# A hybrid encoder layer: attention scores and value products in fewer, larger groups between projection matmuls

## The chip, the cores and the metric

The kernel runs on one core of a Trainium2 chip. The metric is the device time of one execution in microseconds (us), the median of several runs. An execution is profiled too; its times are counted from the start of its span.

## The reference

One post-norm layer over 512 tokens of width 1024: a token mixer of two parallel branches (a bidirectional Mamba-2 SSD, and dilated sliding-window attention), a gated merge, a LayerNorm, then a squared-ReLU channel layer. What matters here is the attention branch: three groups of four heads of 64, with (window, dilation) of (128, 1), (512, 4) and (2048, 16).

```python
u = h @ w_in
z, xbc, dt_f_raw, dt_b_raw, q, k, v, gate_logits = split(u)
y_ssd = ssd_branch(z, xbc, ...) @ w_proj_ssd
y_att = attention_branch(q, k, v) @ w_proj_attn
gates = sigmoid(gate_logits + b_gate)
mix = (gates[:, :, 0] * y_ssd + gates[:, :, 1] * y_att) @ w_out
h = layer_norm(alpha * h + mix, ln1_g, ln1_b)
...
# attention, for each pattern: scores inside the window, softmax, values
scores = einsum(q, k) / sqrt(64) - slope * distance      # masked by the window
m = max(scores); p = exp(scores - m); den = sum(p)
o = einsum(p, v) / den;  lse = m + log(den)
# the j-th heads of the three patterns are combined by softmax(lse)
y = sum(softmax(lse) * o)
```

## The kernel before

Everything is float32. A large product splits its operands into a high and a low float32r half and runs as three matmuls of 128x128 by 128x512; `quarters` (L160) emits the 24 of one such tile, and gives the turn away after every six. Small products (scores, values, transposes) use plain float32, and the profile shows two records for each such matmul, or for a transpose one.

The order on TensorE is written out by hand: `run(a, b, ta, tb)` takes two generators, counts the units that each yields, and steps the one that is behind its share. So a `yield 3.5` in a generator sets how many projection matmuls stand behind that piece. The orders of VectorE, ScalarE and of SP's DMA queue come from a scheduler, in which some helpers (the splits of weights among them, L110 and L111) have a high priority.

In the first stage `ssd(g)`, for g = 0 to 3, runs beside the input projection (tiles ps_z, ps_x, ps_k, ps_g and so on). Each group builds transposes, six states (ps_st, whose running states pv are made by L711), then pauses, runs `norm` of the group before (ps_ms, L592) and four pairs of heads (ps_yo, L760). A pair's gates G are made on ScalarE and VectorE (L731 to L744), and `y_out` of the next group multiplies them (ps_y, L607).

In the second stage `attention()` runs beside the first half of the SSD output projection (ps_pa), 12 tiles of 24 matmuls.

- Scores of the near pattern (L924): per tile i of two heads, four blocks b of 128 queries. The matmuls have 64 rows, and two heads run at once in the two halves of the array.
- Scores of the other two patterns (L954): per tile of two heads four residue classes r. q and k are loaded from DRAM (L877, L878) into two pairs of buffers that alternate.
- Each score tile is read from PSUM once by VectorE (add of the bias, L932 and L958); then follow the maximum, its negative and ScalarE's exponential with the sum (L936, L964).
- The near statistics go through DRAM to another layout (dr_st, L942, and s, L967). Then the three patterns' weights wg are made, and the near ones w0 go through DRAM too.
- Probabilities are scaled by these weights (L998, L1020), transposed by TensorE (`class_t`, L1001; `near_t`, L1025), copied to SBUF, and multiplied with the values (`class_v`, L1012, 64 columns; `near_v`, L1040, 64 columns, at both ends 64 rows too). The products are put in a list `todo`; `later()` emits what stands in it.

PSUM tiles come from three tags: mm (3 banks, for the projections), tp (3) and y (2). A score tile takes two of tp or two of y, one for each head:

```python
        def pair_tiles(n, name):
            tag, bufs = (("tp", 3), ("y", 2))[n]
            return [ps_tile(tag, f"{name}_{hh}", bufs) for hh in range(2)]
```

After the attention, 24 more projection matmuls run before the first product with its result (ps_pb).

Of the kernel before, what the change touches and what calls it, by code (L numbers as in the profile page):

```python
# [16 lines left out]
P = 128  # L17
# [3 lines left out]
NCH = S // P  # L21
HEADS = 32
GROUPS = 4
HD = 64
# [22 lines left out]
def hybrid_layer_kernel(ctx: ExitStack, tc: tile.TileContext, t: dict, out: bass.AP):  # L47
    nc = tc.nc
    act, dve, pool, pe, dma = nc.scalar, nc.vector, nc.gpsimd, nc.tensor, nc.sync
# [133 lines left out]
    def ps_tile(tag, name, bufs):  # L183
        return psp.tile([P, 512], F32, name=name, tag=tag, bufs=bufs)
# [392 lines left out]
    def square_split(g):  # L577

        sqh = sp.tile([P, S], F32R, name=f"sqh{g}", tag="xw", bufs=1)
        sql = sp.tile([P, S], F32R, name=f"sql{g}", tag="G2", bufs=1)  # L580
        act.copy(sqh, tail[g])
        dve.tensor_sub(sql, tail[g], f32(sqh))
        if not onesr:
            onesr.append(cp.tile([P, P], F32R, name="onesr", tag="dtv", bufs=1))
            act.copy(onesr[0], ones)
        sq_hl[g] = sqh, sql
# [55 lines left out]
    def ssd(g):  # L642
# [23 lines left out]
        for c0 in range(0, NCH, 2):  # L666
            pss = [ps_tile("tp", f"ps_xt{g}_{c}", 3) for c in (c0, c0 + 1)]
# [29 lines left out]
        for n, (i, d, c) in enumerate(steps):  # L697
# [16 lines left out]
                gate(ready[n:n + 1])  # L714
            if n == 4 and g:
                square_split(g - 1)
        yield 2.0 if g < GROUPS - 1 else 5.0
        if g:
            norm(g - 1)

# [145 lines left out]
    def attention():  # L866
# [6 lines left out]
        def tile_qk(n):  # L873
            qk[n] = [(ap if n % 2 else aq).tile([P, S], F32, name=f"{x}{n}", tag=f"{x}{n % 2}", bufs=1) for x in "qk"]

        def load_qk(n):
            dma.dma_start(qk[n][0], dr_qk[n])  # L877
            dma.dma_start(qk[n][1], dr_qk[6 + n])  # L878
# [9 lines left out]
        b12 = ap.tile([P, 8, P], F32, name="b12")  # L888
        ptc = {(gg, jj): ap.tile([P, 4, P], F32, name=f"pt{gg}_{jj}") for gg in range(2) for jj in range(4)}
# [10 lines left out]
        b0 = aq.tile([P, 4, 256], F32, name="b0")  # L900
# [5 lines left out]
        kr = [(max(0, P * b - 64), min(S, P * b + 192)) for b in range(NCH)]  # L906
# [3 lines left out]
# [3 lines that stand above are left out]

        for i in range(2):
            qf, kf = qk[i]
            for bp in range(2):
                pss = pair_tiles(bp, f"ps_s0_{i}{bp}")
                for bb in range(2):
                    b = bp * 2 + bb
                    k0, k1 = kr[b]  # L920
                    o = k0 - (P * b - 64)
                    for hh in range(2):
                        pr = slice(hh * HD, (hh + 1) * HD)
                        pe.matmul(pss[hh][:, bb * 256 + o:bb * 256 + o + k1 - k0], qf[pr, b * P:(b + 1) * P], kf[pr, k0:k1], start=True, stop=True)  # L924
                for hh in range(2):
                    jj = 2 * i + hh
                    for bb in range(2):
                        b = bp * 2 + bb
                        k0, k1 = kr[b]
                        w, o = k1 - k0, k0 - (P * b - 64)  # L930
                        pt = pt0[jj, b]
                        dve.tensor_add(pt[:, :w], pss[hh][:, bb * 256 + o:bb * 256 + o + w], b0[:, jj, o:o + w])  # L932
                        dve.reduce_max(st0[:, b, 0, jj:jj + 1], pt[:, :w], axis=AX.X)
                        nm = nm0[:, b, jj:jj + 1]
                        dve.tensor_scalar(nm, st0[:, b, 0, jj:jj + 1], -1.0, None, op0=ALU.mult)
                        act.activation(pt[:, :w], pt[:, :w], AF.Exp, bias=nm, accum_out=st0[:, b, 1, jj:jj + 1])  # L936
                yield 3.5
        dma.dma_start(vc, dr_v.rearrange("(i r) d -> i r d", r=4)[:, :, 0:512])
        dma.dma_start(v0[:, 1:4, :], dr_v[64:448, 512:768].rearrange("(c p) d -> p c d", p=P))
        dma.dma_start(v0[0:64, 0, :], dr_v[0:64, 512:768])  # L940
        dma.dma_start(v0[0:64, 4, :], dr_v[448:512, 512:768])
        dma.dma_start(dr_st.rearrange("(b p) m -> p b m", p=P), st0.rearrange("p b a j -> p b (a j)"))  # L942
        for gg in range(2):
            for i in range(2):
                tl = 2 + gg * 2 + i
                tile_qk(tl)
                load_qk(tl)
                qf, kf = qk[tl]
                pss = pair_tiles(i, f"ps_s{tl}")
                for r in range(4):  # L950
                    rs = slice(r * P, (r + 1) * P)
                    for hh in range(2):
                        pr = slice(hh * HD, (hh + 1) * HD)
                        pe.matmul(pss[hh][:, rs], qf[pr, rs], kf[pr, rs], start=True, stop=True)  # L954
                for hh in range(2):
                    jj = i * 2 + hh
                    pt = ptc[gg, jj]
                    dve.tensor_add(pt, pss[hh].rearrange("p (r k) -> p r k", r=4), b12[:, gg * 4 + jj:gg * 4 + jj + 1, :].to_broadcast([P, 4, P]))  # L958
                    ms = stc[:, gg, 0, :, jj]
                    dve.reduce_max(ms, pt, axis=AX.X)  # L960
                    nm = nmc[:, gg, jj, :]
                    dve.tensor_scalar(nm, ms, -1.0, None, op0=ALU.mult)
                    for r in range(4):
                        act.activation(pt[:, r, :], pt[:, r, :], AF.Exp, bias=nm[:, r:r + 1], accum_out=stc[:, gg, 1, r, jj:jj + 1])  # L964
                yield 4.0

        dma.dma_start(s0, dr_st.rearrange("(i r) (a j) -> i r a j", r=4, a=2))  # L967
        m = [s0[:, :, 0, :], stc[:, 0, 0], stc[:, 1, 0]]
# [19 lines left out]
        def tt_tile(name):  # L988
            nt[0] += 1
            n = nt[0] % 7  # L990
            if n < 4:
                return (aq, ap)[n // 2].tile([P, 4, P], F32, name=name, tag=("q0", "k0", "q1", "k1")[n], bufs=1)
            return ap.tile([P, 4, P], F32, name=name, tag="tt", bufs=3)

        def class_t(i, hh, gg):
            jj = 2 * i + hh
            pt = ptc[gg, jj]
            dve.tensor_mul(pt, pt, wg[:, 1 + gg, :, jj].unsqueeze(2).to_broadcast([P, 4, P]))  # L998
            ps = ps_tile("tp", f"ps_pt{gg}_{jj}", 3)
            for r in range(4):  # L1000
                pe.transpose(ps[:, r * P:(r + 1) * P], pt[:, r, :], ident)  # L1001
            tt = tt_tile(f"tt{gg}_{jj}")
            act.copy(tt.rearrange("p r q -> p (r q)"), ps)
            return tt

        def class_v(i, ptt):
            pcl[i] = ps_tile("y", f"ps_ac{i}", 2)
            for r in range(4):
                for gg in range(2):
                    for hh in range(2):  # L1010
                        v = vc[:, r, (gg * 2 + i) * P + hh * HD:(gg * 2 + i) * P + (hh + 1) * HD]
                        pe.matmul(pcl[i][hh * HD:(hh + 1) * HD, r * P:(r + 1) * P], v, ptt[hh, gg][:, r, :], start=(gg == 0), stop=(gg == 1))  # L1012
# [3 lines left out]
        def near_t(i, b):  # L1016
            w = kr[b][1] - kr[b][0]
            for hh in range(2):
                pt = pt0[2 * i + hh, b]
                dve.tensor_scalar(pt[:, :w], pt[:, :w], w0[:, b, 2 * i + hh:2 * i + hh + 1], None, op0=ALU.mult)  # L1020
            ps = ps_tile("tp", f"ps_pn{i}_{b}", 3)
            tt = tt_tile(f"tn{i}_{b}")
            for hh in range(2):
                for q, (c0, c1, ck) in enumerate(cuts[b]):
                    pe.transpose(ps[:c1 - c0, (q * 2 + hh) * P:(q * 2 + hh + 1) * P], pt0[2 * i + hh, b][:, c0:c1], ident)  # L1025
            if all(c1 - c0 == P for c0, c1, _ in cuts[b]):
                act.copy(tt.rearrange("p r q -> p (r q)"), ps)
            else:
                for q, (c0, c1, ck) in enumerate(cuts[b]):
                    act.copy(tt[:c1 - c0, 2 * q:2 * q + 2, :], ps[:c1 - c0, q * 256:(q + 1) * 256].rearrange("p (h q) -> p h q", h=2))  # L1030
            return tt
# [21 lines left out]
        def later():  # L1053
            while todo:
                todo.pop(0)()

        for i in range(2):
            tts = {}
            for hh in range(2):
                for gg in range(2):  # L1060
                    tts[hh, gg] = class_t(i, hh, gg)
                    yield 1.4
            later()
            todo.append(lambda i=i, tts=tts: class_v(i, tts))
            for b in range(NCH):
                tt = near_t(i, b)
                yield 2.4
                if b == 2:
                    later()
                todo.append(lambda i=i, b=b, tt=tt: near_v(i, b, tt))  # L1070
        later()

# [111 lines left out]
    for k in range(4):  # L1184
        w = ws.get(2)
# [384 lines left out]
    with tc.manual_schedule(engines={mybir.EngineType.PE}):  # L1570
        for c in range(3):
            for q in range(4):
# [9 lines left out]
                pr = product(c, SEQ[2 * q], ops)  # L1582
# [62 lines left out]
    pss = [bank(n, f"ps_d0_{n}") for n in (3, 4, 5, 2)]  # L1645
    for n in range(4):
        w = ws.get()
# [79 lines left out]
```

## Time and profile before

| what | value |
|---|---|
| median of 3 runs | 982.07 us (981.93 to 982.13) |
| profiled execution, its own time | 982.07 us |
| its span, first to last instruction | 980.3 us |
| TensorE clock granted | 0.997 of full speed |
| attention's scores, 483 to 530 us: TensorE / VectorE / ScalarE busy | 47.00 / 42.15 / 29.49 us |
| attention's values, 530 to 576 us: the same | 46.00 / 17.16 / 17.95 us |
| end of the third SSD group's states, 305 to 320 us: the same | 14.74 / 15.00 / 12.45 us |

Matmuls overlap: one of 512 columns is shown with 0.39 us, and the next starts before it ends. So the busy time of TensorE says little of how densely it works, and starts have to be compared. In the timeline a row has the start, the time from the first start to the last end of the instructions merged in it, the engine, the line, the operation with what it writes and reads, and the count; in brackets stand idle time ahead of it and what ended that.

### The profile page before, as it was taken

The numbers are of one execution on the slowest core, as the hardware profiler recorded it, in microseconds if no ns is written. First come the engines' busy times: TensorE is split into PE (matmuls) and PEld (weight loads), VectorE is DVE, ScalarE is ACT, GpSimd is POOL, SyncE is SP. The second block draws the span as 40 slices with busy tenths as digits, with TensorE's granted clock in tenths as the row PEclk, the third lists the DMA queues.
The fourth block names the chain that finished last, engine by engine and source line by source line (L and its number), as shares of the span: only waits on it lengthen the run. The fifth ranks groups of instructions, "written<-read, shape, count | busy, mean of one in ns | idle before, by whom it ended". The sixth has DMA issues, their size and how long they took to land.

```text
span 980.3 us, 14776 instructions
## 1 busy us (share of the span) xinstructions
PE 971.7 (99%) x5448; PEld 835.2 (85%) x5448; DVE 804.6 (82%) x1247; ACT 607.8 (62%) x1150; POOL 58.7 (6%) x67
## 2 busy tenths in 40 slices
PE   9999999999999999999999999999999999999997
PEld 6988888888888888888778888899999998989986
DVE  7987997688999999997798267498898898898757
ACT  6664795469867985784775343157666666656620
POOL 0100200010001000200000000000200110110000
PEclk9999999999999999999999999999999999999998
DMA  9666466334753575474774247313953754671322
GB/s 350 158 146 172 127 207 192 98 103 150 220 162 106 161 216 149 145 232 134 251 230 155 80 153 271 116 44 130 243 143 136 209 130 172 177 167 44 111 83 86
DMA packets 57992, 155.94 MB, mean 159 GB/s; under 512 B 7488, under 2 KB 10432, under 8 KB 57664
## 3 DMA queue, kind: packets, MB, share of 16 engines
q1 hardware_dynamic: 53072, 139.04, 44.0%
q0 software_dynamic: 4560, 15.44, 8.6%
q8 instruction: 43, 0.70, 0.3%
q10 hardware_dynamic: 288, 0.52, 0.2%
q14 instruction: 29, 0.24, 0.1%
HBM read 128.25 MB, written 12.44 MB: 144 GB/s over the span
## 4 chain that ended last, share of the span: by engine, by line
PE 97%; DVE 1%; issue 1%; DMA 0%; ACT 0%; DVEq 0%; SPq 0%; ACTq 0%
PE ps_pa L160 9%; PE ps_g L160 9%; PE ps_x L160 9%; PE ps_z L160 9%; PE ps_x L1366 8%; PE ps_z L1366 4%; PE ps_q L160 3%; PE ps_k L160 3%; PE ps_u L160 2%; PE ps_pX L170 2%; PE ps_pX L171 2%; PE ps_pX L172 2%; PE ps_yo L760 2%; PE ps_y L1366 2%; PE ps_vX L353 2%; PE ps_pZ L170 2%
## 5 line engine op out<-in xcount | busy, mean ns | idle before, releaser
L111 DVE TENSOR_TENSOR wl<-wraw,wh 128x1024 fp32r<-128x1024 f32 x103 | 126.7, 1234 | 64.0 <-ACT wh L110 48.0
L110 ACT CAST wh<-wraw 128x1024 fp32r<-128x1024 f32 x103 | 107.4, 1046 | 86.7 <-PE ps_o L172 14.0
L1482 DVE TENSOR_TENSOR cl<-wq_B,ch 128x1024 fp32r<-128x1024 f32 x42 | 51.3, 1220 | 14.7 <-ACT ch L1481 14.2
L1481 ACT CAST ch<-wq_B 128x1024 fp32r<-128x1024 f32 x42 | 44.1, 1050 | 24.0 <-PE ps_pX L172 16.6
L160 PE MATMUL ps_pa<-yh,wh 128*128 128x512 f32 x128 | 51.7, 404 | 0.0
L160 PE MATMUL ps_g<-xh,wh 128*128 128x512 f32 x128 | 50.6, 396 | 0.0
L160 PE MATMUL ps_z<-xh,wh 128*128 128x512 f32 x128 | 50.4, 394 | 0.0
L160 PE MATMUL ps_g<-xl,wh 128*128 128x512 f32 x128 | 49.9, 390 | 0.0
L160 PE MATMUL ps_z<-xl,wh 128*128 128x512 f32 x128 | 49.9, 389 | 0.0
L160 PE MATMUL ps_pa<-yl,wh 128*128 128x512 f32 x128 | 48.4, 393 | 0.0
L729 ACT ACTIVATE U<-bc,acr 128x128 f32<-128x128 f32 x128 | 42.2, 390 | 8.3 <-DMA bc<-dr_acr 8.3
L160 PE MATMUL ps_x<-xh,wh 128*128 128x512 f32 x120 | 47.3, 394 | 0.0
L160 PE MATMUL ps_x<-xl,wh 128*128 128x512 f32 x120 | 46.8, 390 | 0.0
L525 DVE SCALAR_TENSOR_TENSOR acc<-ps_x,vec,acc 128x510 f32<-128x510 f32 (+1 forms) x60 | 44.6, 743 | 0.5
L1450 POOL DMA_DIRECT2D wq_B<-wq_B x24 | 20.6, 856 | 402.3 <-DMA wq_B<-in_w_dn_dram 236.4
L731 DVE SCALAR_TENSOR_TENSOR U<-bc,acr,U 128x128 f32<-128x128 f32 x128 | 44.0, 381 | 0.0
L735 ACT ACTIVATE G<-cb,tok 128x128 f32<-128x128 f32 x128 | 41.9, 390 | 0.0
L170 PE MATMUL ps_pX<-ch,ah 128*128 128x512 f32 x96 | 37.6, 392 | 0.0
L171 PE MATMUL ps_pX<-cl,ah 128*128 128x512 f32 x96 | 37.6, 392 | 0.0
L172 PE MATMUL ps_pX<-ch,al 128*128 128x512 f32 x96 | 37.4, 389 | 0.0
L1475 ACT CAST ah<-r 128x1024 fp32r<-128x1024 f32 x21 | 22.1, 1054 | 20.6 <-PE ps_pX L171 14.3
L160 PE MATMUL ps_pa<-yh,wl 128*128 128x512 f32 x128 | 34.8, 392 | 0.0
(884 smaller groups left out, 2825.5 us busy)
## 6 DMA issues: line engine op xcount, KB each, us to landing
wraw<-in_w_in_dram SPq DMA_DIRECT2D x66, 512.0 KB, 3.9
bc<-dr_acr SPq DMA_DIRECT2D x64, 256.0 KB, 4.2
pr<-in_w_up_dram SPq DMA_DIRECT2D x28, 512.0 KB, 5.4
wq_B<-in_w_dn_dram SPq DMA_DIRECT2D x24, 512.0 KB, 4.4
wq_B<-wq_B POOLq DMA_DIRECT2D x24, 512.0 KB, 4.6
be<-dr_ear SPq DMA_DIRECT2D x32, 256.0 KB, 5.3
wraw<-in_w_ps_dram SPq DMA_DIRECT2D x16, 512.0 KB, 3.7
dr_gate<-g SPq DMA_DIRECT2D x16, 256.0 KB, 2.3
```

Of the source, the lines that this page charges most:

```text
L110: a = act.copy(h[:, :width], r[:, :width])
L111: v = dve.tensor_sub(l[:, :width], r[:, :width], f32(h[:, :width]))
L160: ins = pe.matmul(ps, l, r, start=(first and n == 0), stop=(last and n == len(seq) - 1))
L170: pe.matmul(ps, lh, rh, start=(first and i == 0), stop=False, skip_group_check=not check)
L171: pe.matmul(ps, lh, rl, start=False, stop=False, skip_group_check=not check)
L172: ins = pe.matmul(ps, ll, rh, start=False, stop=(last and i == n - 1), skip_group_check=not check)
L525: dve.scalar_tensor_tensor(acc[:, o0:o1], ps[:, i0:i1], w(k), acc[:, o0:o1], op0=ALU.mult, op1=ALU.add)
L729: act.activation(U[:, ch(c)], bb[:, ch(c)], AF.Identity, bias=acr[:, c, 32 + h:33 + h])
L731: dve.scalar_tensor_tensor(U[:, ch(c)], bf[:, ch(c)], acr[:, c, h:h + 1], U[:, ch(c)], op0=ALU.subtract, op1=ALU.min)
L1366: pe.matmul(ps[:, LO], w_[:, wk], src[:, x, k0 + k, cs], start=(first and i == 0), stop=(i == 11), skip_group_check=not first)
L1481: act.copy(h, w[:, j, :])
L1482: dve.tensor_sub(l, w[:, j, :], f32(h))
```

## The change

Four edits. The near scores of one tile are emitted as one group of eight matmuls into four PSUM tiles (before: two groups of four), and the scores of two tiles of the other patterns as one group of 16 (before: two groups of eight). The value products are emitted at two places (before: four): all those of tile 0 behind the second pair of class transposes of tile 1, all those of tile 1 at the end. So that the transposed near blocks can wait that long, they are copied into probability tiles ptc that have been transposed already, not into the rotating tiles. And the pause of the third SSD group is 3.4 units, not 2.0. Line numbers behind the first edit of `attention` move by up to three: the scores are L922 and L956 in the changed kernel.

```diff
-        yield 2.0 if g < GROUPS - 1 else 5.0
+        yield (2.0, 2.0, 3.4, 5.0)[g]
         if g:
             norm(g - 1)
...
         for i in range(2):
             qf, kf = qk[i]
+            pss = [pair_tiles(bp, f"ps_s0_{i}{bp}") for bp in range(2)]
+            for b in range(NCH):
+                k0, k1 = kr[b]
+                o = (b % 2) * 256 + k0 - (P * b - 64)
+                for hh in range(2):
+                    pr = slice(hh * HD, (hh + 1) * HD)
+                    pe.matmul(pss[b // 2][hh][:, o:o + k1 - k0], qf[pr, b * P:(b + 1) * P], kf[pr, k0:k1], start=True, stop=True)
             for bp in range(2):
-                pss = pair_tiles(bp, f"ps_s0_{i}{bp}")
...
-                yield 3.5
+            yield (10.0, 6.5)[i]
...
         for gg in range(2):
+            pss = []
             for i in range(2):
                 tl = 2 + gg * 2 + i
                 tile_qk(tl)
                 load_qk(tl)
+            for i in range(2):
+                tl = 2 + gg * 2 + i
                 qf, kf = qk[tl]
-                pss = pair_tiles(i, f"ps_s{tl}")
+                pss.append(pair_tiles(i, f"ps_s{tl}"))
...
-                yield 4.0
+            yield (8.0, 5.5)[gg]
...
-            tt = tt_tile(f"tn{i}_{b}")
+            tt = ptc[b // 2, 2 * i + b % 2]
...
                 for gg in range(2):
                     tts[hh, gg] = class_t(i, hh, gg)
                     yield 1.4
-            later()
+                if hh == 0:
+                    later()
             todo.append(lambda i=i, tts=tts: class_v(i, tts))
             for b in range(NCH):
                 tt = near_t(i, b)
                 yield 2.4
-                if b == 2:
-                    later()
                 todo.append(lambda i=i, b=b, tt=tt: near_v(i, b, tt))
         later()
```

What this does to the order is shown at three places. First TensorE at the first near scores. Before, four matmuls stand between projection matmuls (ps_s_00 names tile 0, block pair 0, and the last digit the head):

```order
L160 MATMUL ps_pa_4939<-yl_4818,wh_4925 128x512
L924 MATMUL ps_s_00_0_4958<-k_4916,q_4915 128x192
L924 MATMUL ps_s_00_1_4959<-k_4916,q_4915 128x192
L924 MATMUL ps_s_00_0_4958<-k_4916,q_4915 128x256
L924 MATMUL ps_s_00_1_4959<-k_4916,q_4915 128x256
L160 MATMUL ps_pa_4939<-yl_4821,wh_4925 128x512
```

The same place of TensorE in the changed kernel:

```order
L160 MATMUL ps_pa_4939<-yl_4818,wh_4925 128x512
L922 MATMUL ps_s_00_0_4958<-k_4916,q_4915 128x192
L922 MATMUL ps_s_00_1_4959<-k_4916,q_4915 128x192
L922 MATMUL ps_s_00_0_4958<-k_4916,q_4915 128x256
L922 MATMUL ps_s_00_1_4959<-k_4916,q_4915 128x256
L922 MATMUL ps_s_01_0_4960<-k_4916,q_4915 128x256
L922 MATMUL ps_s_01_1_4961<-k_4916,q_4915 128x256
L922 MATMUL ps_s_01_0_4960<-k_4916,q_4915 128x192
L922 MATMUL ps_s_01_1_4961<-k_4916,q_4915 128x192
L160 MATMUL ps_pa_4939<-yl_4821,wh_4925 128x512
```

Block pair 1 has joined pair 0. Before, the eight groups have 12, 18, 12, 12, 18, 18, 12 and 54 projection matmuls behind them; now the four have 42, 24, 30 and 60.

Second, TensorE at the pause of the third SSD group, before:

```order
L160 MATMUL ps_C_3070<-xh_103,wl_2999 128x512
L592 MATMUL ps_ms_3122<-sqh_3084,onesr 128x512
L592 MATMUL ps_ms_3122<-sql_3085,onesr 128x512
L760 MATMUL ps_yo_0_3135<-C_2194,pv_0_1_2929 128x128
L760 MATMUL ps_yo_0_3135<-C_2194,pv_0_2_3013 128x128
L760 MATMUL ps_yo_0_3135<-C_2194,pv_0_3_3081 128x128
L760 MATMUL ps_yo_1_3136<-C_2194,pv_1_0_3104 128x128
```

And in the changed kernel:

```order
L160 MATMUL ps_C_3070<-xh_103,wl_2999 128x512
L160 MATMUL ps_z_3128<-xh_96,wh_3066 128x512
L160 MATMUL ps_z_3128<-xl_104,wh_3066 128x512
L160 MATMUL ps_z_3128<-xh_97,wh_3066 128x512
L160 MATMUL ps_z_3128<-xl_105,wh_3066 128x512
L160 MATMUL ps_z_3128<-xh_98,wh_3066 128x512
L160 MATMUL ps_z_3128<-xl_106,wh_3066 128x512
L592 MATMUL ps_ms_3135<-sqh_3084,onesr 128x512
L592 MATMUL ps_ms_3135<-sql_3085,onesr 128x512
L760 MATMUL ps_yo_0_3148<-C_2194,pv_0_1_2929 128x128
```

Six matmuls of the next z tile have moved ahead of ps_ms and ps_yo; the later pairs of heads of this group move by six too.

Third, VectorE while it reads the first near scores (st is the maximum, nm its negative, wl a weight's low half), before:

```order
L111 TENSOR_TENSOR wl_4989<-wraw_4931,wh_4988 128x1024
L933 TENSOR_REDUCE st_4905<-pt_01_4876 128x1
L932 TENSOR_TENSOR pt_10_4879<-ps_s_00_1_4959,b_4914 128x192
L935 TENSOR_SCALAR nm_4907<-st_4905 128x1
L932 TENSOR_TENSOR pt_11_4880<-ps_s_00_1_4959,b_4914 128x256
L933 TENSOR_REDUCE st_4905<-pt_10_4879 128x1
L933 TENSOR_REDUCE st_4905<-pt_11_4880 128x1
```

And in the changed kernel:

```order
L932 TENSOR_REDUCE st_4905<-pt_01_4876 128x1
L931 TENSOR_TENSOR pt_10_4879<-ps_s_00_1_4959,b_4914 128x192
L934 TENSOR_SCALAR nm_4907<-st_4905 128x1
L931 TENSOR_TENSOR pt_11_4880<-ps_s_00_1_4959,b_4914 128x256
L932 TENSOR_REDUCE st_4905<-pt_10_4879 128x1
L111 TENSOR_TENSOR wl_5011<-wraw_4931,wh_5010 128x1024
L934 TENSOR_SCALAR nm_4907<-st_4905 128x1
L932 TENSOR_REDUCE st_4905<-pt_11_4880 128x1
```

The split of the weight has moved behind the reads of this pair. The adds behind it (block pair 1) keep their order, and the next two splits move in the same way by a few rows.

More of the change, by code (lines that the diff above doesn't have):

```diff
@@ L915, in attention @@
             qf, kf = qk[i]
-            for bp in range(2):
-                pss = pair_tiles(bp, f"ps_s0_{i}{bp}")
[L918 to L924, printed above, removed]
+            pss = [pair_tiles(bp, f"ps_s0_{i}{bp}") for bp in range(2)]
[5 more added lines that the diff above has]
+                    pe.matmul(pss[b // 2][hh][:, o:o + k1 - k0], qf[pr, b * P:(b + 1) * P], kf[pr, k0:k1], start=True, stop=True)
+            for bp in range(2):
                 for hh in range(2):
@@ L931, in attention @@
                         pt = pt0[jj, b]
-                        dve.tensor_add(pt[:, :w], pss[hh][:, bb * 256 + o:bb * 256 + o + w], b0[:, jj, o:o + w])
+                        dve.tensor_add(pt[:, :w], pss[bp][hh][:, bb * 256 + o:bb * 256 + o + w], b0[:, jj, o:o + w])
                         dve.reduce_max(st0[:, b, 0, jj:jj + 1], pt[:, :w], axis=AX.X)
@@ L953, in attention @@
                         pr = slice(hh * HD, (hh + 1) * HD)
-                        pe.matmul(pss[hh][:, rs], qf[pr, rs], kf[pr, rs], start=True, stop=True)
+                        pe.matmul(pss[i][hh][:, rs], qf[pr, rs], kf[pr, rs], start=True, stop=True)
+            for i in range(2):
                 for hh in range(2):
@@ L957, in attention @@
                     pt = ptc[gg, jj]
-                    dve.tensor_add(pt, pss[hh].rearrange("p (r k) -> p r k", r=4), b12[:, gg * 4 + jj:gg * 4 + jj + 1, :].to_broadcast([P, 4, P]))
+                    dve.tensor_add(pt, pss[i][hh].rearrange("p (r k) -> p r k", r=4), b12[:, gg * 4 + jj:gg * 4 + jj + 1, :].to_broadcast([P, 4, P]))
                     ms = stc[:, gg, 0, :, jj]
```

## The prediction

> **What bounds the kernel now.** I read the page first, then the list of waits for TensorE alone, then TensorE's timeline around each place that the change touches.
>
> ```profile
> PE 971.7 (99%) x5448; PEld 835.2 (85%) x5448; DVE 804.6 (82%) x1247; ACT 607.8 (62%) x1150; POOL 58.7 (6%) x67
> ```
>
> TensorE is busy for 99% of the span. The list of its waits has two entries:
>
> ```profile
> PE ps_warm L235 <- DVE warm L232: 1.2, 1, 1.2
> PE ps_yo L760 <- DVE pv L711: 0.3, 1, 0.3
> ```
>
> So outside the start TensorE hardly waits. What can be won lies inside "busy": a matmul that starts later than its neighbours' pitch allows counts as busy. The pitch must be read from starts. The timeline of TensorE around one group of scores (start, duration, line, count):
>
> ```profile
> 498.36 1.98 PE L160 MATMUL ps_pa<-yh,wl 128*128 128x512 f32 x8
> 500.27 1.16 PE L954 MATMUL ps_s<-k,q 64*128 64x128 f32 x16
> 501.36 0.50 PE L160 MATMUL ps_pa<-yh,wh 128*128 128x512 f32 x1
> 501.70 0.39 PE L160 MATMUL ps_pa<-yh,wl 128*128 128x512 f32 x1
> ...
> 502.86 0.39 PE L160 MATMUL ps_pa<-yh,wh 128*128 128x512 f32 x1
> ...
> 505.12 0.61 PE L160 MATMUL ps_pa<-yl,wh 128*128 128x512 f32 x2
> ```
>
> Undisturbed, ten projection matmuls go from 502.86 to 505.12: 0.227 us each. From 498.36 to 502.86 there are 4.50 us with 14 of them (3.18), so the 16 score records, which run as 8 pairs, cost 1.32. What a pair costs by itself shows in the middle of the group:
>
> ```profile
> 500.60 0.60 PE L954 MATMUL ps_s<-k,q 64*128 64x128 f32 x6
> ...
> 501.04 0.39 PE L954 MATMUL ps_s<-k,q 64*128 64x128 f32 x4
> ```
>
> The second row starts four pairs after the first and 0.44 us later: 0.11 a pair. Eight pairs are 0.88; the other 0.44 us belong to going in and coming out. Coming out is plain in the rows: 0.34 between 501.36 and 501.70 in place of 0.227.
>
> **The change, part by part.**
>
> *Scores in four groups.* The first two tiles have shorter groups:
>
> ```profile
> 482.76 0.62 PE L160 MATMUL ps_pa<-yl,wh 128*128 128x512 f32 x2
> 483.31 1.03 PE L924 MATMUL ps_s<-k,q 64*128 64x192 f32 x8
> 484.26 1.65 PE L160 MATMUL ps_pa<-yl,wh 128*128 128x512 f32 x6
> 485.75 0.39 PE L160 MATMUL ps_pa<-yh,wh 128*128 128x512 f32 x1
> ```
>
> 2.99 us less 8 x 0.227 leaves 1.17. Two pairs of 192 and two of 256 columns at 0.11 per 128 are 0.77, so 0.40 is the price of the excursion. No matmul is removed; the eight groups become four, so two prices of 0.40 and two of 0.44 go: **1.68 us**. The bounds: nothing, if the seam inside a merged group costs as much as the excursion that it replaces, and 1.7, if it costs nothing. I take the upper one, since pairs inside a group already alternate between operands and PSUM banks, as the seam does, and run at 0.11.
>
> *Value products in two groups.* One of the four groups of before starts and ends at projection matmuls; another follows transposes of single blocks:
>
> ```profile
> 542.84 1.97 PE L1012 MATMUL ps_ac<-tt,vc 128*64 128x128 f32 x32
> 544.74 1.24 PE L1040 MATMUL ps_an<-tn,v 64*64 64x128 f32 x16
> 545.91 0.66 PE L1025 MATMUL ps_pn<-ident,pt 128*128 128x128 f32 x4
> ...
> 568.98 0.86 PE L160 MATMUL ps_pa<-yh,wl 128*128 128x512 f32 x3
> 569.76 1.24 PE L1040 MATMUL ps_an<-tn,v 128*64 128x128 f32 x16
> 570.94 0.50 PE L160 MATMUL ps_pa<-yh,wh 128*128 128x512 f32 x1
> 571.27 0.40 PE L160 MATMUL ps_pa<-yl,wh 128*128 128x512 f32 x1
> ```
>
> Going in: the third projection matmul starts at 569.44 (568.98 and two pitches), the first product 0.32 later, 0.10 over the pitch. The 32 records of L1012 are 16 pairs; their last starts 1.70 after the first (1.97 less the 0.27 of one), 0.05 over 15 x 0.11. Coming out to transposes: 545.91 is 0.21 after the last pair (544.74 + 1.24 - 0.27 = 545.71), again 0.10 over, and the four transposes take 0.06 more than 3 x 0.11. So about 0.15 for each change. Two groups of four go, with an entry and an exit each: 4 x 0.15 = **0.6 us**; bounds 0.4 (the first gaps alone) and 0.75. The blocks that keep the array's shape, and the change from 128 rows to 64 inside a product, remain. The block transposes stand in the same count of excursions, 15.
>
> *Dead probability tiles for the transposed blocks.* The copy out of PSUM is the same ScalarE instruction to another address. Zero; it allows the products to wait so long. The class tiles that are written there before had their transposes long ago, and the eighth class tile takes a buffer that the merged products have just read.
>
> *Pause of the third SSD group.* Around the one wait of the list:
>
> ```profile
> 315.04 0.39 PE L592 MATMUL ps_ms<-sqh,onesr 128*128 128x512 f32 x1
> ...
> 315.50 0.83 PE L760 MATMUL ps_yo<-C,pv 128*128 128x128 f32 x6
> 316.58 0.94 PE L760 MATMUL ps_yo<-C,pv 128*128 128x128 f32 x6 [0.26 <-DVE pv L711]
> ...
> 310.23 2.06 DVE L111 TENSOR_TENSOR wl<-wraw,wh 128x1024 fp32r<-128x1024 f32 x1
> ...
> 314.01 1.91 DVE L731 SCALAR_TENSOR_TENSOR U<-bc,acr,U 128x128 f32<-128x128 f32 x7
> 315.85 0.67 DVE L711 TENSOR_TENSOR pv<-pv,ps_st 128x512 f32<-128x512 f32 x1
> ```
>
> The seventh ps_yo record was due at 315.50 + 6 x 0.11 = 316.16 and starts at 316.58, when the last pv (315.85 + 0.67) is written: 0.42 us. The six records from there take 0.94 in place of 0.83: 0.11 more. Six matmuls of the next z tile now stand ahead of ps_ms, 6 x 0.227 = 1.36 us, so the record is due at 317.5, 1.0 after pv. **0.5 us** goes. VectorE's order up to this pv is unchanged, and the split of z's weights, the first of these VectorE rows, is done at 312.29. What comes 1.36 later relative to the projection are the four heads' ps_yo; their gates have much room: the last gate of this group is done at 372.56, its product starts at 380.05.
>
> ```profile
> 371.88 0.68 DVE L744 TENSOR_TENSOR G<-G,U 128x512 f32<-128x512 f32 x1
> ...
> 380.05 3.71 PE L607 MATMUL ps_y<-G,xt 128*64 128x128 f32 x64
> ```
>
> *What the merged groups wait for.* Group two needs all four PSUM tiles of group one, which VectorE must have read:
>
> ```profile
> 494.51 0.34 DVE L932 TENSOR_TENSOR pt<-ps_s,b 128x192 f32<-128x192 f32 x1
> ...
> 495.36 1.21 DVE L111 TENSOR_TENSOR wl<-wraw,wh 128x1024 fp32r<-128x1024 f32 x1
> ```
>
> Before, the last read ends at 494.85. The new order has the same VectorE instructions up to it, with the weight split a few rows later, so the same 494.85. TensorE: group one starts at 483.31 as before, lasts 2 x 0.77 + 0.2, then come 42 projection matmuls (9.53) and the exit's 0.13: group two starts at 494.7 and writes the second pair of tiles 0.87 later, at 495.6. Margin 0.7 us. Group three follows 1.75 + 24 x 0.227 later, at 502.1; VectorE's reads for it end at about 501.3.
>
> Groups three and four also need tiles of q and k that load into buffers which the group before frees. SP's queue, then the time to landing of the line that loads k (L878) and of the store (L942):
>
> ```profile
> 497.46 0.32 SPq L877 DMA_DIRECT2D q<-dr_qk  x1
> 497.83 0.42 SPq L878 DMA_DIRECT2D k<-dr_qk  x1
> 503.15 0.37 SPq L942 DMA_DIRECT2D dr_st<-st  x1
> ...
> DMA to landing us min/median/max: 3.3/4.2/5.5
> ...
> DMA to landing us min/median/max: 1.8/1.8/1.8
> ```
>
> The third tile's k leaves at 497.8 again, lands at 502.0, and is wanted at 503.2, since its half is the second of group three. The fifth tile's loads stand behind the store dr_st, which waits for the near scores' last exponential. A weight split (1.2 us, the L111 row above) now stands ahead of that one's maximum, so the store leaves at 504.4; s waits for its landing, 1.8 us, and takes 0.4 of the queue, then come q and k: k leaves at 507.0, lands at 511.2. It is wanted at 512.1: group three ends at 504.1, its exit costs 0.13, 30 projection matmuls 6.8, and the fifth tile is the second half of group four, 1.0 later. With the slowest landing, 5.5, the two are 0.1 and 0.4 late. I take no wait.
>
> Behind group four stands the softmax:
>
> ```profile
> 515.11 1.16 PE L954 MATMUL ps_s<-k,q 64*128 64x128 f32 x16
> ...
> 525.19 3.10 DVE L998 TENSOR_TENSOR pt<-pt,wg 128x512 f32<-128x512 f32 x5
> ...
> 528.58 0.60 PE L1001 MATMUL ps_pt<-ident,pt 128*128 128x128 f32 x4
> ```
>
> Now 528.58 - (525.19 + 0.68) leaves 2.7 us. The last group ends at 513.1, 3.2 us before the old end of 516.3, but leaves four tiles of 512 columns to add, reduce and exponentiate in place of two, some 2.5 us of VectorE; the first transposes come 1.7 earlier, at 526.9. About 1.7 us remain.
>
> **Sum.** 1.68 + 0.6 + 0.5 = 2.8 us, all on TensorE's own chain, with nothing behind it that waits. The profiled execution took 982.07, its span 980.3; it is the median of the runs shown too. 982.07 - 2.8 = **979.3 us**.
>
> [...]
>
> **Rivals.**
> *Only the gaps at the change go.* Of a score excursion's 0.42, 0.09 at the entry and 0.10 at the exit are the change itself; the slow first pair and the second projection matmul's 0.11 could belong to new operands and come back at the seam. Then 4 x 0.19 + 4 x 0.10 + 0.5 = 1.7: 980.4. Against it: operands change within groups at no cost. 0.1.
> *The merged groups wait.* One or two of the thin margins (0.7 for PSUM, 1.1 and 0.9 for k) turn into waits of 0.2 to 1 us: 979.7 to 981. For it: the margins are a tenth of the distance between groups, and VectorE runs back to back through the rows at 494.51 to 495.36. 0.15.
> *Slower.* PSUM emptying sets the pace: all four score tiles are now full at once, where before two emptied while two filled. If VectorE's 16 score tiles ran late by more than 0.7 + 2.8, as when the yl splits (L859) ahead of them slip, group two would wait and each later group with it; at 6 us late the time is 984.6. It decides from 3.5 us, and shows as slower from 5.5. [...] 0.04.
> *The pause does nothing* (pv slips by as much): 979.8, still faster. 0.05.
>
> **Chances and range.** Forecast 0.66. Such a measurement can tell about 0.2%, 2.0 us, from no change: faster means below 980.1, slower above 984.0. Forecast, the idle pause, and half of the waiting groups: faster 0.79. The other half, and the gaps-only rival: same 0.17. Slower 0.04. The bounds of the terms (products 0.4 to 0.75, scores down to half) with waits up to 1 us give 978.8 to 981.0.
>
> **What would show it.** Right: four groups of 16 score records with one slow first pair each; two value groups; no wait of ps_yo on pv; no new entry of more than 0.1 in TensorE's waits. Wrong: ps_s waiting for a pt of VectorE or for a k load, ps_pt for pt, or ps_pb for atl, whose chain behind the last product is unchanged; or a seam of more than 0.11 in a group.

## The result, and the profile after

The changed kernel takes 979.87 us (median of 12 executions, 979.17 to 981.41; before, on the same chip, 982.0): a ratio of 0.9978, interval 0.9971 to 0.9986. That is faster by 0.2%, 2.1 us where 2.8 were forecast, and the interval leaves out 1. The profiled execution took 979.88 with a span of 977.9.

Of the page the row of TensorE, and its whole list of waits (total, count, longest), both after:

```profile
PE 968.8 (99%) x5448; PEld 835.6 (85%) x5448; DVE 804.4 (82%) x1247; ACT 609.2 (62%) x1150; POOL 59.5 (6%) x67
```

```profile
PE ps_warm L235 <- DVE warm L232: 1.2, 1, 1.2
PE ps_B L300 <- ACT xh L145: 0.9, 1, 0.9
```

The wait of ps_yo has gone. A new one has come where nothing was changed: ps_B, in the first projection tiles, waits for ScalarE's cast of a block of x, and ScalarE waits for that block to land:

```profile
7.00 1.92 ACT L145 CAST xh<-xr 128x512 fp32r<-128x512 f32 x3 [1.03 <-DMA xr<-in_xT_dram]
```

TensorE's starts, read stage by stage in the two timelines, say where the time went:

| stage on TensorE (first start to first start, us) | before | after | difference | forecast |
|---|---|---|---|---|
| span's start to the first transposes of SSD group 0 | 73.01 | 73.32 | +0.31 | 0 |
| from there to the first score (pause within) | 410.30 | 409.76 | -0.54 | -0.5 |
| scores, to the first transposes of probabilities | 45.27 | 43.66 | -1.61 | -1.68 |
| values, to the first ps_pb | 47.93 | 47.33 | -0.60 | -0.6 |
| ps_pb to the end | 403.78 | 403.79 | 0 | 0 |

So the three steps gave 2.75 of 2.8, and this execution lost 0.31 at its start: its span is 2.4 shorter. Its own time fell by 2.2 only, since the part of it outside the span is 2.0 here and was 1.8 before.

TensorE's timeline after, around group three of the scores:

```profile
501.68 0.39 PE L160 MATMUL ps_pa<-yh,wl 128*128 128x512 f32 x1
502.00 2.06 PE L956 MATMUL ps_s<-k,q 64*128 64x128 f32 x32
503.99 0.50 PE L160 MATMUL ps_pa<-yh,wh 128*128 128x512 f32 x1
504.32 0.39 PE L160 MATMUL ps_pa<-yh,wl 128*128 128x512 f32 x1
```

From 501.68 to 504.32 are 2.64 us with two projection matmuls (0.45) and 16 pairs (1.78): 0.41 is left, about the price that before was paid for 8 pairs (0.44). The 17th record is the first of the second tile; the row that begins with it:

```profile
503.00 0.39 PE L956 MATMUL ps_s<-k,q 64*128 64x128 f32 x4
```

It starts 1.00 after the first. A slow first pair of 0.21 and seven pitches of 0.11 make 0.98, so the seam between the two tiles costs nothing.

The place of the pause, after:

```profile
316.49 0.39 PE L160 MATMUL ps_z<-xl,wh 128*128 128x512 f32 x1
316.72 0.39 PE L592 MATMUL ps_ms<-sqh,onesr 128*128 128x512 f32 x1
...
317.17 1.50 PE L760 MATMUL ps_yo<-C,pv 128*128 128x128 f32 x12
318.43 0.48 PE L160 MATMUL ps_z<-xh,wh 128*128 128x512 f32 x1
```

The twelve ps_yo records run through; before, they stood in two pieces with a wait between them.

Two thin margins can be read too: VectorE's last read of group one, and SP's load of k for the second half of group three, with its time to landing:

```profile
494.27 0.34 DVE L931 TENSOR_TENSOR pt<-ps_s,b 128x192 f32<-128x192 f32 x1
```

```profile
497.22 0.42 SPq L878 DMA_DIRECT2D k<-dr_qk  x1
...
DMA to landing us min/median/max: 4.9/4.9/4.9
```

Group two starts at 494.58 and needs that tile some 0.8 later, at 495.4, where the read has ended at 494.6. k lands at 502.2 and is wanted at 503.0. Both hold here, the second by 0.8. Tiles are counted from 0, as in the prediction: this is the k of tile 3, which the prediction calls the third.

### The profile page after: what moved, and what is told of

Read it like the earlier page. It is cut to its first block, busy times and chain, and to the rows that moved or that the text cites. A ratio compares the mean times of both kernels' runs of the same rounds, so it can differ in the third digit from the quotient of the medians.

```text
span 977.9 us, 14765 instructions
## 1 busy us (share of the span) xinstructions
PE 968.8 (99%) x5448; PEld 835.6 (85%) x5448; DVE 804.4 (82%) x1247; ACT 609.2 (62%) x1150; POOL 59.5 (6%) x67
## 4 chain that ended last, share of the span: by engine, by line
PE 99%; DMA 1%; DVE 0%; SPq 0%; DVEq 0%; ACT 0%; issue 0%
PE ps_pa L160 9%; PE ps_g L160 9%; PE ps_x L160 9%; PE ps_z L160 9%; PE ps_x L1368 8%; PE ps_z L1368 4%; PE ps_k L160 3%; PE ps_q L160 3%; PE ps_u L160 2%; PE ps_pX L170 2%; PE ps_pX L171 2%; PE ps_pX L172 2%; PE ps_yo L760 2%; PE ps_y L1368 2%; PE ps_vX L353 2%; PE ps_pZ L171 2%
## 6 DMA issues: line engine op xcount, KB each, us to landing
wraw<-in_w_in_dram SPq DMA_DIRECT2D x66, 512.0 KB, 3.8
pr<-in_w_up_dram SPq DMA_DIRECT2D x28, 512.0 KB, 5.4
wq_B<-in_w_dn_dram SPq DMA_DIRECT2D x24, 512.0 KB, 4.4
wq_B<-wq_B POOLq DMA_DIRECT2D x24, 512.0 KB, 4.7
wraw<-in_w_ps_dram SPq DMA_DIRECT2D x16, 512.0 KB, 3.7
```

## Experiments

The median of before is 981.95 to 982.03 in all comparisons. An excursion is what the prediction calls the way from the projection matmuls into a group of small ones and back.

**Scores alone** (e1_scores). The kernel before with the two score loops of the change:

```diff
+            pss = [pair_tiles(bp, f"ps_s0_{i}{bp}") for bp in range(2)]
...
+            yield (10.0, 6.5)[i]
...
+            yield (8.0, 5.5)[gg]
```

> The kernel before with the scores in four groups, and nothing else of the change. Theory (each of the four excursions saved was worth its whole 0.40 to 0.44 us, and a merged group has no price at its seam): 1.6 to 1.7 us less, about 980.4 if before is 982.05; from the first score record to the first transposes of the probabilities TensorE needs 1.6 less than before's 45.3, and the 16 pairs of a merged group stand 0.11 apart right through. Rival (only the gaps at the change of shape go, the slow first pair comes back at the seam): 0.8 less, 981.3, and one pair in the middle of a group is 0.1 to 0.2 late. Rival (the merged groups wait for PSUM or for k): any gain, but with a wait of ps_s on pt or on a load in TensorE's list of waits.

Measured 980.98 (980.48 to 981.91; ratio 0.9990, 0.9981 to 0.9998): 1.05 us less, not 1.65. In its profile the scores are shorter by 0.83 only. TensorE's timeline at group three, and the load of k for its second half:

```profile
502.54 1.16 PE L956 MATMUL ps_s<-k,q 64*128 64x128 f32 x16
504.22 1.16 PE L956 MATMUL ps_s<-k,q 64*128 64x128 f32 x16 [0.52 <-DMA k<-dr_qk]
```

```profile
497.77 0.42 SPq L878 DMA_DIRECT2D k<-dr_qk  x1
...
DMA to landing us min/median/max: 6.4/6.4/6.4
```

k landed at 504.13, 0.59 after it was wanted (502.54 and 1.0). That is the rival "the merged groups wait", here in full: 0.59 and 0.2 more are the 0.78 that the scores lack to the 1.61 of the changed kernel.

**Values alone** (e2_values). The kernel before with the products at two places:

```diff
-            tt = tt_tile(f"tn{i}_{b}")
+            tt = ptc[b // 2, 2 * i + b % 2]
...
+                if hh == 0:
+                    later()
```

> The kernel before with the value products in two groups and the blocks' transposes in dead probability tiles, and nothing else of the change. Theory (0.15 at each change between projection matmuls or transposes and products, four changes fewer): 0.6 us less, 981.45; from the first transposes of the probabilities to ps_pb 47.3 instead of before's 47.9. Rival (the first gap alone, 0.10 each): 0.4 less. Rival (the copies into the probability tiles, or products that wait for them, cost what is won): no difference, and a wait of ps_an or ps_pt shows.

In the profile 0.60 less between the first transposes and ps_pb, no new wait: the theory's figure. The median was 981.48, 0.55 less; but three of eleven executions lay at 982.5 to 984.2, so the ratio says nothing (1.0001, 0.9992 to 1.0009), and the gain rests on the profile.

**Pause alone** (e3_pause).

```diff
-        yield 2.0 if g < GROUPS - 1 else 5.0
+        yield (2.0, 2.0, 3.4, 5.0)[g]
```

> The kernel before with the pause of the third SSD group at 3.4, and nothing else of the change. Theory (ps_yo's wait for pv goes with its 0.42 us and the slow pitch of 0.11 behind it): 0.5 us less, 981.5; no wait of ps_yo in TensorE's list. Rival (pv or a later product slips by as much): no difference, and ps_yo or ps_y waits elsewhere.

Median 981.23 (981.12 to 981.51), 0.8 less; ratio 0.9993 (0.9984 to 1.0001). The interval holds 1, so this gain too rests on the profile: there the stage with the pause gave 0.54 and the start 0.32. No wait but that of ps_warm is left.

**The change again, twice** (e4_again, e12_again; no edit).

> The changed kernel once more, word for word. Its first profile lost 0.3 us before the v stage, where ps_B waited 0.9 for a block of x to land; the instructions there are those of before. Theory (the landing of the first x blocks varies from execution to execution, whatever the kernel): in this execution the wait is another, and the profile's own time follows it: 979.3 to 979.9, by the start alone, with the same 2.7 to 2.8 us gained behind the start. Rival (the change itself delays the start): ps_B waits 0.9 again, here and not in the three other kernels of this batch, and the time is 979.9.

> The changed kernel a third time, beside the two with early loads. Theory (late k in part of the executions): in the profile k of the third tile lands between 0.8 before and 0.8 after its use; where it is late, ps_s waits for it and the scores take as much longer; median 0.3 to 0.6 above the kernel with the early loads. Rival (k is no part of it): the same median as the kernel with the early loads.

979.70 both times (978.87 to 983.17 and 979.14 to 980.72). In the first, ps_B waited 0.7 and still the start cost nothing (73.0 to the first transposes); pause, scores and values gave 0.54, 1.61 and 0.60. In the second the scores gave 1.07 only: k left at 496.92, landed 6.1 later, at 503.04, and was wanted at 502.68. TensorE's timeline there:

```profile
501.68 1.16 PE L956 MATMUL ps_s<-k,q 64*128 64x128 f32 x16
503.13 1.16 PE L956 MATMUL ps_s<-k,q 64*128 64x128 f32 x16 [0.28 <-issue]
```

The second row starts 0.45 later than 1.0 after the first. The view names "issue" for this wait, not the load; that it is the load is read from the landing 0.09 ahead of the start, and from e1_scores, where the same wait is put down to k. So the same program meets the late k in some executions and not in others.

**Finer groups** (e5_split). The kernel before with a pause between the two blocks of a pair:

```diff
+                    if bb == 0:
+                        yield 1.0
...
-                yield 3.5
+                yield 2.5
```

> The kernel before with the near scores cut finer: every block's four records by themselves, six projection matmuls between two blocks of a pair, so twelve groups of scores instead of eight; the sum of the pauses is that of before. Theory (each excursion has a price of its own, 0.40 for near scores): four more cost 1.6 us, 983.6; from the first score record to the first transposes 46.9 instead of before's 45.3. Rival (only the gaps of 0.09 and 0.10 belong to an excursion, the rest to new operands that come anyway): 0.8 more, 982.8.

One of the four new pauses brought no projection matmul between its blocks (the turn went back at once), so there were three excursions more, eleven groups. The scores took 1.30 longer, 0.43 for each; the time was 983.18 (982.95 to 983.61; ratio 1.0011, 1.0002 to 1.0020). For three, the theory says 1.2 and the rival 0.6. TensorE's timeline of this kernel at a block of 256 columns that stands by itself now:

```profile
485.10 0.40 PE L160 MATMUL ps_pa<-yl,wh 128*128 128x512 f32 x1
485.42 0.70 PE L924 MATMUL ps_s<-k,q 64*128 64x256 f32 x4
486.06 0.50 PE L160 MATMUL ps_pa<-yh,wh 128*128 128x512 f32 x1
486.39 0.39 PE L160 MATMUL ps_pa<-yl,wh 128*128 128x512 f32 x1
```

The entry takes 0.32 where the pitch is 0.227. Two pairs of 256 columns, 0.43 by themselves, take 0.64 to the next projection matmul, and the second of those starts 0.33 after the first: entry, slow first pair, exit and slow second matmul are all paid again.

**Rows filled up** (e6_pad). The changed kernel, without products of 64 rows:

```diff
...
+        dma.dma_start(v0[64:128, 0, :], dr_v[0:64, 512:768])
+        pool.memset(v0[0:64, 0, :], 0.0)
+        pool.memset(v0[64:128, 4, :], 0.0)
+        for jj in range(4):
+            pool.memset(pt0[jj, 0][:, 0:64], 0.0)
+            pool.memset(pt0[jj, 3][:, 192:256], 0.0)
...
+        cuts = [[(0, 128, b), (128, 256, b + 1)] for b in range(NCH)]
...
```

> The changed kernel with the near products of 64 rows filled up to 128: the outer blocks' probabilities and the values at both ends are kept beside 64 columns or rows of zeros, so that all value products have 128 rows (eight memsets on GpSimd of probabilities, two of values; the output is that of before). Theory (a change of the row count inside the products costs 0.15, as a change between shapes does; three of them in each of the two groups go): 0.9 us less than the changed kernel, about 978.9 beside 979.8; a value group lasts 3.65 from its first record to its last instead of 4.1. Rival (128 rows to 64 keeps the pipeline full, the 0.15 belong to the operands): no difference. Rival (the memsets or the full transposes cost it again): no difference, with a wait of ps_pn or ps_an.

978.92 (978.35 to 979.64; ratio 0.9969, 0.9956 to 0.9981). The values are 1.48 shorter than before's, 0.88 more than the change. The first group of products, in the changed kernel and here:

```profile
547.85 1.97 PE L1015 MATMUL ps_ac<-tt,vc 128*64 128x128 f32 x32
549.75 2.26 PE L1043 MATMUL ps_an<-pt,v 64*64 64x128 f32 x32
551.94 0.66 PE L1004 MATMUL ps_pt<-ident,pt 128*128 128x128 f32 x4
```

```profile
547.96 1.97 PE L1020 MATMUL ps_ac<-tt,vc 128*64 128x128 f32 x32
549.76 1.92 PE L1048 MATMUL ps_an<-pt,v 128*64 128x128 f32 x32
551.61 0.66 PE L1009 MATMUL ps_pt<-ident,pt 128*128 128x128 f32 x4
```

4.09 became 3.65: three changes of row count, 0.15 each. (k was late in this profile as well: it landed at 502.90 and was wanted at 502.34, and the scores gave 0.85.)

**Group two earlier** (e8_early).

```diff
-            yield (10.0, 6.5)[i]
+            yield (9.0, 7.5)[i]
```

> The changed kernel with the second group of scores six projection matmuls (1.36 us) earlier, the others where they were. Theory (PSUM emptying is the limit: VectorE's last read of the first group ends 0.84 us before the second group writes that pair of tiles): ps_s waits 0.5 us for pt, and the time is 0.5 more than the changed kernel's, about 980.3. Rival (the tiles are free much earlier than VectorE's rows say): no wait, no difference.

980.12 (979.66 to 980.68), 0.4 over the changed kernel's 979.70, which was measured on other chips; in the profile the scores lose 0.66. TensorE at group two and VectorE's last read of group one:

```profile
493.26 2.49 PE L922 MATMUL ps_s<-k,q 64*128 64x192 f32 x16
...
494.34 0.38 PE L922 MATMUL ps_s<-k,q 64*128 64x256 f32 x1
...
494.73 0.48 PE L922 MATMUL ps_s<-k,q 64*128 64x256 f32 x2
...
495.68 0.50 PE L160 MATMUL ps_pa<-yh,wh 128*128 128x512 f32 x1
```

```profile
494.31 0.36 DVE L931 TENSOR_TENSOR pt<-ps_s,b 128x192 f32<-128x192 f32 x1
```

The group takes 2.42 to the next projection matmul, and 1.72 in the changed kernel. The list of waits shows none of this. The two records of the first head's third block, whose PSUM tile is free (VectorE's last read of it ended at 493.36), ran on alone, the second at 494.34; the second head's records of that block, and the rest of the group with them, came from 494.73 on, behind the read that ends at 494.67. So PSUM's emptying does limit, some 0.7 us off, as the prediction had it; "no wait in the list" didn't mean "no wait".

**Other buffers** (e9_buf). In the changed kernel the q and k of tile 3 load into the spare buffers of the transposes, and those of tiles 4 and 5 into the buffers of tiles 1 and 2:

```diff
+            if n == 3:
+                qk[n] = [ap.tile([P, 4, P], F32, name=f"{x}{n}", tag="tt", bufs=3).rearrange("p r q -> p (r q)") for x in "qk"]
...
```

> The changed kernel with other buffers for q and k of the later tiles: the third tile uses two buffers that are empty until the transposes, the fourth and fifth those of two groups before, so that their loads leave SP earlier. Theory (the k of the third tile lands 0.2 to 0.8 us before its use, and in some executions after it, which costs the changed kernel a few tenths): k lands over 1.5 us before its use in every group, no ps_s waits for a load, the highest runs lie within 0.8 of the lowest, and the median is 0.1 to 0.5 below the changed kernel's, 979.3 to 979.7. Rival (the spread of the changed kernel comes from the start or from elsewhere): median and spread stay, 979.8 and some executions above 982.

979.34 (979.05 to 979.9), as the theory said, but not by its mechanism: k left at 496.24, 1.0 earlier than in the first profile and only 0.5 earlier ahead of its use, since SP still had it behind a load of a weight, issued at 495.87. It landed 6.3 later, at 502.49, just when it was wanted, and the scores gave 1.40. So this run doesn't show that the other buffers help.

**Early loads** (e11_early; its text counts tiles from one). q and k of tiles 2 and 3 load at the start of the attention, into probability tiles of the last group:

```diff
+            if n in (2, 3):
+                qk[n] = [ptc[1, 2 * n - 4 + m].rearrange("p r q -> p (r q)") for m in range(2)]
...
+        for n in (2, 3):
+            tile_qk(n)
+            load_qk(n)
...
```

> The changed kernel with q and k of the third and fourth tile loaded at the start of the attention, into four probability tiles that are empty until the last group of scores; the fifth and sixth tile then load into the buffers of the first two. Theory (what the changed kernel lacks to the forecast is the late k of group three, on top of a start that varies by some 0.4 either way): k of group three lands over 5 us and that of group four over 3 us before use, no ps_s waits for a load, from the first score record to the first transposes TensorE needs 1.6 less than before's 45.3 in this profile as in any, and the median is 979.2 (before 982.0 less 2.75), the runs within 0.8 of each other. Rival (the rest of the spread is elsewhere): median 979.7, some executions above 981.

979.29 (979.01 to 979.67; ratio 0.9974, 0.9963 to 0.9984): 2.70 less than before, 0.41 less than the changed kernel beside it. k landed at 492.2, ten us ahead; the scores gave 1.61.

**Both** (e10_best). Early loads and filled rows together.

> The early loads and the value products filled up to 128 rows in one kernel (zeros as before, the output is that of before). Theory (both gains are TensorE's own time and add): 0.9 less than the kernel with the early loads alone, 978.3; scores 1.6 and values 1.5 shorter than before's. Rival (GpSimd's memsets or the fuller DMA queue take it back): 979.2 and a wait of ps_s, ps_pn or ps_an.

978.21 (978.05 to 978.79; ratio 0.9964, 0.9951 to 0.9976), the fastest of all: 3.8 us less than before. Its scores gave 1.62, its values 1.48.

The load that decides, over all profiles with merged groups (us; what the scores lose is against 1.61):

| kernel | k leaves | lands | wanted | late by | scores lose |
|---|---|---|---|---|---|
| changed, first profile | 497.22 | 502.17 | 503.00 | -0.83 | 0 |
| e4_again | 496.90 | 502.45 | 502.67 | -0.22 | 0 |
| e9_buf | 496.24 | 502.49 | 502.50 | -0.01 | 0.21 |
| e12_again | 496.92 | 503.04 | 502.68 | +0.36 | 0.54 |
| e6_pad | 496.57 | 502.90 | 502.34 | +0.56 | 0.76 |
| e1_scores | 497.77 | 504.13 | 503.54 | +0.59 | 0.78 |
| e8_early | 497.28 | 502.87 | 503.70 | -0.83 | 0.66 (PSUM) |
| e11_early | 485.42 | 492.23 | 502.50 | -10.3 | 0 |
| e10_best | 486.24 | 492.46 | 502.64 | -10.2 | 0 |

Wanted is 1.0 after the group's first record. Where k is late, or lands just as it is wanted, the scores lose the lateness and 0.2. Before the change the same k was wanted at 505.67, 3.5 us after it landed.

## Why the prediction was right, and where it missed

- **Scores, 1.68.** Right in kind and size: 1.61 or 1.62 in every profile in which PSUM was empty in time and k landed at least 0.2 ahead of its use. The choice between the whole excursion (0.42) and its gaps alone (0.19) is settled by the finer groups, 0.43 each. The rival "only the gaps at the change go" falls.
- **Values, 0.6.** 0.60 in all profiles with the merged products and their 64-row ends. What the prediction called the remaining change inside a product, from 128 rows to 64, was worth 0.15 each time too, and could be had.
- **Pause, 0.5.** 0.54, alone and with the rest; "the pause does nothing" falls.
- **PSUM margin, 0.7.** Right: the rows of the changed kernel give 0.8, and it broke when 1.36 us were taken away, at a cost of 0.66.
- **"I take no wait."** This is the step that failed. The prediction took 4.2 us for k's landing and held 5.5 for the slowest, which would have been 0.1 late. With the groups moved together the load took 4.9 to 6.4. So the rival given 0.15, "the merged groups wait", is not an alternative but happens in part of the executions, 0.2 to 0.8 us each; e12_again shows the prediction's own sign of being wrong, a ps_s that waits for a k load. That the first profile has no such wait is luck of that execution. Taking the wait away is worth 0.41 on the median, and brings the time to the forecast (979.29 against 979.3). The other margin held by luck in part: k of tile 5 left at 507.7, not 507.0, and landed 0.8 ahead of its use (511.2 against 512.0) because it took 3.5; with the 4.2 of the forecast 0.1 would have been left. And the terms given for group three, 1.75 and 24 pitches from 494.7 on, make 501.9, not the 502.1 stated; measured are 7.42 from group to group, so only the figure was right.
- **The start** was not in the forecast. Up to the first transposes of SSD group 0, thirteen profiles took 72.66 to 73.36, before's 73.01 and the change's 73.32 among them, with the same instructions. It varies by 0.35 either way, and makes 0.31 of the first profile's shortfall. That the change delays the start is ruled out by its own two repeats (72.99 and 73.00).
- **Outside the span.** This was not in the forecast either. The own times lie above the spans by 1.79 to 1.81 on the mean of the executions in before, e1_scores, e3_pause and e5_split, and by 1.86 to 2.02 in every kernel with the new value products. So 0.1 to 0.2 us of the gain are lost outside the span, in all kernels that have that edit and in none without; why is not known.
- Left open: five of the 35 executions of the changed kernel, and two of e2_values, lay 1.5 to 3.5 us above their medians, none of those with the scores or the pause alone. Four of the five and both of e2_values are from one chip; the 36 executions of the variants of the changed kernel, on two others, have none. No profile caught one.

## What to carry to other kernels

Price an excursion from TensorE's starts, at both ends and one instruction deeper (0.40 to 0.44 us here), and see at the seam whether merged groups save it whole, as they did here (the 17th record 1.00 after the first, 0.98 without a seam). Merging also brought demands forward (k was wanted at 503.00, before at 505.67): for each load whose use moves up, compare the old slack (3.5 us here) with the spread of landings (4.9 to 6.4), not with their median, and where buffers that are still empty can take the load, start it early (k then landed 10.3 ahead of its use, e11_early). A change of the row count inside the run of value products cost 0.15 us here, as a change between shapes did; filling up with zeros took 0.44 off a group (e6_pad).

## What was not expected of the hardware

- A load of 256 KB that landed 4.2 to 4.5 us after its issue in before, e2_values and e3_pause took 4.9 to 6.4 in the kernels with merged groups and no early load, where SP issues it closer behind a 512 KB load of a weight (0.86 us in the changed kernel, 1.24 before). That this distance is the cause was not tried by itself, and it can't be all: k took 4.9, 5.6 and 6.1 in three profiles of one program with the same 0.86, and the load of the weight ahead of it was slow with it (4.5, 5.2 and 5.7, against 3.6 to 4.5 in before, e2_values and e3_pause).
- In the value products 128 to 64 rows and back cost 0.15 us each (0.44 for three, e6_pad against the changed kernel), as much as going from projection matmuls to products (0.10 at the first gap and 0.05 at the first pair, before).
- In the changed kernel the score records of the two heads start 0.007 us apart at most, pair by pair. In e8_early one head waited and the other ran on alone for a block: its second record of 256 columns came at 494.34, 0.22 after the first as an estimate (the first stands 0.86 behind the start of the group in the changed kernel, so at 494.12 here). That is as slow as the pair, 0.22 in the changed kernel, and the wait is in no list.
